# Two early loads of a convolution moved from SyncE's DMA queue to ScalarE's, behind a one-column copy

## The chip, the core and the metric

The kernel runs on one core of one Trainium2 chip. A core has five engines with instruction streams of their own: TensorE (PE; its weight loads are shown as PEld), VectorE (DVE), ScalarE (ACT), GpSimd (POOL) and SyncE (SP). TensorE multiplies and writes its results to PSUM; the others work elementwise or start transfers between HBM and SBUF. A DMA that an engine starts stands in that engine's queue; the transfers themselves run on 16 DMA engines. The metric is the device time of one execution in microseconds (us), lower is better.

## The reference

The input `x` is 16 x 64 x 64 x 64 (batch, channels in, height, width) in float32, the weight 128 x 64 x 3 x 3. Computed is a 3x3 convolution with a border of zeros, and behind it the maximum over blocks of 2 x 2:

```python
x_pad = np.pad(x, ((0, 0), (0, 0), (pad, pad), (pad, pad)))
for b, co, ci, kh, kw:
    conv[b, co] += weight[co, ci, kh, kw] * x_pad[b, ci, kh:kh+h, kw:kw+w]
for b, c, i, j:
    output[b, c, i, j] = np.max(conv[b, c, 2*i:2*i+2, 2*j:2*j+2])
```

The output is 16 x 128 x 32 x 32 in float32.

## The kernel before, in words

Two images lie in the 128 partitions at a time: 2 x 64 input channels. A matmul uses 64 partitions as its contraction, so matmuls for the two images run in pairs, on the two halves of TensorE's rows. The work is cut into 32 steps; a step is 16 rows of two images, hence 8 rows of pooled output, and each step has two halves `h`, one per image.

For two neighbouring rows the kernel doesn't compute both convolutions as they stand. It uses sums and differences of rows and of taps (the three weights of one row of the 3x3 window), so that fewer products are needed. There are two ways to do so. In a K step the differences are taken of the taps (D2 and D0) and TensorE reads the rows themselves in bfloat16 (`kx`) and a row sum (`ks`). In a W step differences of rows are made (`we` and `wd`, on VectorE or GpSimd) and a row sum `ws`, all from float32 rows in `wx`. Step 0 is a K step, step 1 a W step, step 2 a K step, step 3 a W step.

**The start.** Before a product can run, the weights must be loaded (`wraw`), combined and cast to bfloat16 (`wq`), turned by TensorE's transposes (lines 170) and copied back from PSUM to SBUF (`wt`, lines 182 to 188). The rows of step 0 are loaded as float32 into `kfirst` in two pieces: rows 0 to 8 (line 119) and rows 9 to 16 (line 120). ScalarE casts them to bfloat16 into `kx` (line 492). The first product of step 0 runs in two halves to match: F.0.0 needs the first piece, F.0.1 the second. `ksecond` (line 126) has the rows of step 2, cast at line 501. Step 1, the first W step, has its rows loaded in two parts by `wload(1, 0)` and `wload(1, 1)` (line 112); its differences `we` are made by halves too (Ea and Eb, line 393), and its `wd` at line 408. All these loads are issued by SP, in this order: wraw, kfirst's first piece, kfirst's second piece, ksecond, the two parts of step 1's rows. While they are under way TensorE runs eight matmuls on constants (line 595), whose results nobody reads.

**The order.** The order of instructions on every engine is written out by hand in the string `ORDER`: a name, a step and a half at a time (`EV` copies an accumulator out of PSUM, `MX` takes the maximum of two rows, `OD` copies the odd columns, `CM` takes the maximum of columns, `ST` stores, `L` loads rows, `LB` loads them behind the last VectorE instruction, `LK` loads rows for K steps by GpSimd's queue). Each engine executes its instructions in that order. On ScalarE the beginning is: cast of g0, casts of kfirst (XOa of the first piece; XOb and XEb of the second), a copy of turned taps (VG0), another cast of the first piece (XEa). On TensorE it is: transposes, F.0.0, F.0.1, transposes of D0, F.1.0, F.1.1, F.2.0 and so on. The instructions ahead of `ORDER` (the loads above, the memsets) come first on their engines. ScalarE's activation table is loaded by an instruction that the compiler puts ahead of ScalarE's first computation, which is the cast at line 194.

Of the kernel before, what the change touches and what calls it, by code (L numbers as in the profile page):

```python
# [11 lines left out]
def kernel(  # L12
# [9 lines left out]
    nc = tc.nc  # L22
    FP32 = mybir.dt.float32
    BF16 = mybir.dt.bfloat16
# [29 lines left out]
    const = ctx.enter_context(tc.tile_pool(name="const", bufs=1))  # L54
# [33 lines left out]
    def rows_of(p, lo, hi):  # L88
        return x[2 * p : 2 * p + 2].rearrange("b c h w -> (b c) h w")[:, lo:hi, :]

    def chunk(q):
        return (2 * R * q + (q > 0), min(H, 2 * R * (q + 1) + 1))

    NWX = 3
    kx = {}
    wx = [const.tile([128, H + 2, W], FP32, name=f"wx_{i}") for i in range(NWX)]
# [6 lines left out]
    def wload(s, part=None):  # L103
        p, q = place[s]
        lo, hi = chunk(q)
        if s == WSTEPS[0] and q > 0:
            lo = 2 * R * q - 1
        if part == 0:
            hi = 2 * R * q + R + 1
        elif part == 1:  # L110
            lo = 2 * R * q + R + 1
        return nc.sync.dma_start(out=wx[p % NWX][:, lo + 1 : hi + 1, :], in_=rows_of(p, lo, hi))

    wraw = const.tile([CO, CI * K * K], FP32)
    nc.sync.dma_start(out=wraw, in_=weight.rearrange("a b c d -> a (b c d)"))  # L115
    _, khi = chunk(0)
    kmid = R + 1
    kfirst = const.tile([128, khi, W], FP32)
    nc.sync.dma_start(out=kfirst[:, 0:kmid, :], in_=rows_of(0, 0, kmid))  # L119
    nc.sync.dma_start(out=kfirst[:, kmid:khi, :], in_=rows_of(0, kmid, khi))  # L120
    klo2, khi2 = chunk(1)
    ksecond = const.tile([128, khi2 - klo2, W], FP32)
    first_loads = (2, 1,)
    for s in first_loads:
        if s == KSTEPS[1]:
            nc.sync.dma_start(out=ksecond, in_=rows_of(0, klo2, khi2))
        else:
            wload(s, 0)
            wload(s, 1)
    zeros = const.tile([128, 512], BF16)  # L130
    nc.vector.memset(zeros, 0.0)
    ident = const.tile([128, 128], BF16)
    make_identity(nc, ident)
    for t in wx:
# [295 lines left out]
    def late_load(s):  # L430
        behind(wload(s), sbuf_op[0])
# [206 lines left out]
```

## Time and profile before

| | us |
|---|---|
| median of three runs | 104.66 (104.28 to 104.88) |
| the profiled execution | 104.47 |
| its span | 102.7 |
| TensorE busy | 96.2 (94% of the span) |
| VectorE, ScalarE, GpSimd busy | 91.6, 85.5, 77.9 |

The profile is one execution. Its span runs from the first to the last instruction that is shown; the 1.8 us between the span and the time of the execution lie around it. A line such as L492 is the line of the kernel that issued the instruction. SPq, ACTq and POOLq are the engines' DMA issues. In the list of DMA issues the last number is the time from the start of the issue until the data have landed, as the waiting instruction sees it. "Idle before" is time in which the engine stood still ahead of an instruction, with the event that ended it. TensorE's granted clock was full (1.00) in this profile throughout.

### The profile page before, as it was taken

How to read it: one execution, taken by the hardware profiler on the slowest of the kernel's cores; microseconds unless marked ns; L12 is line 12 of the kernel's file. 1: busy time of each engine (PE TensorE's matmuls, PEld its weight loads, DVE VectorE, ACT ScalarE, POOL GpSimd, SP SyncE). 2: the span in 40 equal slices, each digit the busy share in tenths (PEclk: the TensorE clock that was granted, in tenths of full speed). 3: DMA queues.
4: the chain of work that ended last, by engine and by line, in shares of the span. 5: the costliest groups of instructions: out<-in, count | busy, mean ns of one | idle time of the engine just before them, and what ended most of it. 6: DMA issues, size and time to landing. Idle time of an engine off the chain costs nothing.

```text
span 102.7 us, 2522 instructions
## 1 busy us (share of the span) xinstructions
PE 96.2 (94%) x905; PEld 54.3 (53%) x905; DVE 91.6 (89%) x176; ACT 85.5 (83%) x192; POOL 77.9 (76%) x66
## 2 busy tenths in 40 slices
PE   6969999999999999999999999999999999999920
PEld 2355465444454447655655555567657765555500
DVE  1576979999999999999999989999999999899960
ACT  4278697999889999997998899897989899897830
POOL 6262889995998799489959999789999688990000
PEclk9999999999999999999999999999999999999999
DMA  2989999999999999600538989930803673386553
GB/s 53 286 295 333 281 325 360 362 421 410 293 311 410 311 308 396 220 6 0 175 57 119 245 259 404 389 111 0 307 3 112 216 165 113 106 295 222 208 192 114
DMA packets 13341, 23.60 MB, mean 230 GB/s; under 512 B 1040, under 2 KB 9360, under 8 KB 13328
## 3 DMA queue, kind: packets, MB, share of 16 engines
q1 hardware_dynamic: 12464, 21.20, 58.8%
q0 software_dynamic: 720, 2.10, 11.6%
q8 instruction: 7, 0.11, 0.5%
q10 hardware_dynamic: 144, 0.13, 0.4%
q14 instruction: 6, 0.05, 0.1%
HBM read 17.14 MB, written 8.39 MB: 249 GB/s over the span
## 4 chain that ended last, share of the span: by engine, by line
PE 88%; DMA 4%; DVE 2%; SPq 1%; issue 1%; ACT 0%; DVEq 0%
PE acc L219 86%; DMA kfirst<-in_x_dram 4%; DVE o L477 1%; PE acc L170 1%; DVE acc L467 1%; PE acc L460 1%; SPq L119 0%; ACT kx L492 0%; SPq L115 0%; DVEq L633 0%
## 5 line engine op out<-in xcount | busy, mean ns | idle before, releaser
L219 PEld LDWEIGHTS <-wt 64*128 64x128 bf16 x870 | 51.7, 94 | 39.0 <-issue 2.0
L219 PE MATMUL acc<-wd,wt 64*128 64x504 bf16 (+3 forms) x276 | 54.4, 367 | 0.0
L381 POOL TENSOR_TENSOR wd<-wx 128x1024 bf16<-128x1024 f32 x21 | 49.2, 2360 | 4.5 <-DVE ws L360 2.0
L219 PE MATMUL acc<-kx,wt 64*128 64x504 bf16 (+6 forms) x264 | 44.7, 355 | 0.9 <-DVE wq L508 0.7
L467 DVE TENSOR_TENSOR acc<-acc,ev 128x512 f32<-128x512 f32 x64 | 42.0, 691 | 1.2 <-ACT ev L441 0.7
L219 PE MATMUL acc<-we,wt 64*128 64x512 bf16 (+3 forms) x138 | 32.5, 367 | 0.0
L219 PE MATMUL acc<-ws,wt 64*128 64x512 bf16 (+1 forms) x132 | 32.5, 377 | 0.0
L441 ACT ACTIVATE ev<-acc 128x512 f32<-128x512 f32 x44 | 26.3, 614 | 1.8 <-PE acc L219 1.3
L451 ACT COPY acc<-acc 128x512 f32<-128x512 f32 x42 | 24.5, 591 | 3.0 <-PE acc L219 1.8
L477 DVE TENSOR_TENSOR o<-acc,od 128x256 f32<-128x256 f32 x64 | 24.7, 416 | 0.9 <-ACT od L471 0.9
L471 ACT COPY od<-acc 128x256 f32<-128x256 f32 x64 | 22.8, 382 | 2.2 <-PE acc L219 1.7
L372 POOL TENSOR_TENSOR we<-wx 128x512 bf16<-128x512 f32 x16 | 20.1, 1272 | 4.0 <-PE acc L219 2.4
L219 PE MATMUL acc<-ks,wt 64*128 64x504 bf16 (+1 forms) x60 | 13.7, 377 | 0.0
L439 ACT COPY ev<-acc 128x512 f32<-128x512 f32 x20 | 11.7, 593 | 1.3 <-PE acc L219 1.2
L352 DVE TENSOR_REDUCE ws<-wx 128x512 bf16<-128x1024 f32 x9 | 11.1, 1232 | 0.0
L360 DVE TENSOR_TENSOR ws<-wx 128x512 bf16<-128x512 f32 x7 | 5.3, 766 | 0.0
L320 DVE TENSOR_TENSOR ks<-kx 128x512 bf16<-128x512 bf16 x10 | 4.3, 435 | 0.0
L408 POOL TENSOR_TENSOR wd<-wx 128x512 bf16<-128x512 f32 x2 | 2.5, 1264 | 2.2 <-DVE we L393 2.2
L339 DVE TENSOR_TENSOR ws<-wx,acc 128x512 bf16<-128x512 f32 x6 | 4.1, 675 | 0.0
L595 PE MATMUL acc<-const-bfloat16-1.0 128*128 128x512 bf16 x8 | 3.3, 582 | 0.8 <-PEq L619 0.8
L335 ACT COPY acc<-wx 128x512 f32<-128x512 f32 x6 | 3.6, 598 | 0.1
L372 DVE TENSOR_TENSOR we<-wx 128x512 bf16<-128x512 f32 x4 | 2.9, 749 | 0.3 <-DMA wx<-in_x_dram 0.3
(33 smaller groups left out, 26.6 us busy)
## 6 DMA issues: line engine op xcount, KB each, us to landing
out_dram<-o SPq DMA_DIRECT2D x31, 256.0 KB, 2.9
wx<-in_x_dram SPq DMA_DIRECT2D x10, 512.0 KB, 10.6
wx<-in_x_dram SPq DMA_DIRECT2D x6, 480.0 KB, 9.7
wx<-in_x_dram SPq DMA_DIRECT2D x5, 544.0 KB, 8.5
kx<-in_x_dram POOLq DMA_DIRECT2D x2, 528.0 KB, 7.5
ksecond<-in_x_dram SPq DMA_DIRECT2D x1, 512.0 KB, 6.4
kx<-in_x_dram POOLq DMA_DIRECT2D x1, 496.0 KB, 8.1
wx<-in_x_dram SPq DMA_DIRECT2D x1, 320.0 KB, 6.7
```

What stands on the lines that cost most here:

```text
L219: nc.tensor.matmul(acc[t][:, i0:i1, o0:o1], wt[lo : lo + CI, tap_of(m0, kw, h), :], rows(lo, i0, i1, c0, c1), start=start and kw == 1, sto ...
L320: nc.vector.tensor_tensor(out=row["ks", s], in0=t[:, f : f + 2 * R : 2, :], in1=t[:, f + 1 : f + 2 * R : 2, :], op=ADD)
L352: nc.vector.tensor_reduce(out=row["ws", s], in_=t[:, f : f + 2 * R, :].rearrange("p (r two) w -> p r w two", two=2), axis=mybir.AxisListTy ...
L360: nc.vector.tensor_tensor(out=row["ws", s], in0=t[:, f : f + 2 * R : 2, :], in1=t[:, f + 1 : f + 2 * R : 2, :], op=ADD)
L372: inst = (nc.vector if vector else nc.gpsimd).tensor_tensor(out=row["we", s], in0=t[:, f : f + 2 * R : 2, :], in1=t[:, f + 1 : f + 2 * R : ...
L381: nc.gpsimd.tensor_tensor(out=row["wd", s], in0=t[:, f + 1 : f + 1 + 2 * R, :], in1=t[:, f - 1 : f - 1 + 2 * R, :], op=SUB)
L439: nc.scalar.copy(out=ev[s, h], in_=acc[t])
L441: nc.scalar.mul(ev[s, h], acc[t], -1.0)
L451: nc.scalar.copy(out=acc[t], in_=acc[ta[s, h]])
L467: nc.vector.tensor_tensor(out=t, in0=t, in1=ev[s, h], op=MAX)
L471: nc.scalar.copy(out=od[s, h], in_=acc[tb[s, h]][:, :, 1::2])
L477: nc.vector.tensor_tensor(out=ot[s][:, h], in0=acc[t][:, :, 0::2], in1=od[s, h], op=MAX)
```

## The change

The second piece of `kfirst` and the first part of step 1's rows are issued by ScalarE in place of SP. Ahead of these two issues ScalarE gets a copy of one column of a constant into a tile that nobody reads, so the load of its table stands ahead of that copy and of the two issues. The memset of `zeros` on VectorE is moved to the front of the program. SP then issues wraw, kfirst's first piece, ksecond and the second part of step 1's rows. `ORDER` is unchanged, and so is the order of the computing instructions on every engine but for the added copy.

```diff
         elif part == 1:
             lo = 2 * R * q + R + 1
-        return nc.sync.dma_start(out=wx[p % NWX][:, lo + 1 : hi + 1, :], in_=rows_of(p, lo, hi))
-
+        queue = nc.scalar if part == 0 else nc.sync
+        return queue.dma_start(out=wx[p % NWX][:, lo + 1 : hi + 1, :], in_=rows_of(p, lo, hi))
+
+    zeros = const.tile([128, 512], BF16)
+    nc.vector.memset(zeros, 0.0)
+    primed = const.tile([128, 1], BF16)
+    nc.scalar.copy(out=primed, in_=nc.const_aps.tensor(1.0, [128, 1], BF16))
     wraw = const.tile([CO, CI * K * K], FP32)
     nc.sync.dma_start(out=wraw, in_=weight.rearrange("a b c d -> a (b c d)"))
     _, khi = chunk(0)
     kmid = R + 1
     kfirst = const.tile([128, khi, W], FP32)
     nc.sync.dma_start(out=kfirst[:, 0:kmid, :], in_=rows_of(0, 0, kmid))
-    nc.sync.dma_start(out=kfirst[:, kmid:khi, :], in_=rows_of(0, kmid, khi))
+    nc.scalar.dma_start(out=kfirst[:, kmid:khi, :], in_=rows_of(0, kmid, khi))
     klo2, khi2 = chunk(1)
     ksecond = const.tile([128, khi2 - klo2, W], FP32)
     first_loads = (2, 1,)
...
             wload(s, 0)
             wload(s, 1)
-    zeros = const.tile([128, 512], BF16)
-    nc.vector.memset(zeros, 0.0)
     ident = const.tile([128, 128], BF16)
     make_identity(nc, ident)
```

## The prediction

> **What bounds the kernel now.** I read the waits of TensorE (PE) first, because PE is busy 94% of the span and the question is only where it is not. Columns: who waited for what, total us, times, longest.
>
> ```profile
> PE acc L595 <- PEq L619: 0.8, 1, 0.8
> PE acc L219 <- DVE wq L508: 0.7, 1, 0.7
> PE acc L170 <- DVE wq L507: 0.2, 1, 0.2
> PE acc L219 <- ACT kx L492: 0.2, 1, 0.2
> ```
>
> Four waits, and no more in the whole run. Next I read the chain of work that ended last, for where they lie (start us, us, what).
>
> ```profile
> 1.65 4.30 DMA kfirst<-in_x_dram
> ...
> 5.98 0.41 ACT kx L492
> ...
> 6.43 0.50 PE acc L219 x6
> ...
> 12.27 84.18 PE acc L219 x785
> ```
>
> The chain goes through the second piece of kfirst: issued by SP at 1.65, landed 4.30 later at 5.95, cast by ScalarE (ACT) until 6.39, and the matmuls F.0.1 start at 6.43. Behind that PE never waits again. So whatever moves 6.43 moves the end by the same amount, as long as nothing later runs out of slack, and what stands before it costs nothing. The change touches exactly this stretch, so I read the start as a timeline (start, us, engine, line, what, idle before it):
>
> ```profile
> 0.74 1.28 ACT L194 ACT_TABLE_LOAD   x1 [0.74 <-PEq L619]
> ...
> 1.65 0.42 SPq L120 DMA_DIRECT2D kfirst<-in_x_dram  x1
> ...
> 2.11 0.43 SPq L126 DMA_DIRECT2D ksecond<-in_x_dram  x1
> 2.59 11.01 SPq L112 DMA_DIRECT2D wx<-in_x_dram  x11
> ...
> 3.59 0.53 ACT L194 CAST wq<-wraw 128x192 bf16<-128x192 f32 x1 [1.57 <-DMA wraw<-in_weight_dram]
> ...
> 4.24 0.83 PE L170 MATMUL acc<-ident,wq 128*128 128x128 bf16 x12 [0.19 <-DVE wq L507]
> ...
> 4.66 0.42 DVE L188 COPY wt<-acc 128x512 bf16<-128x512 bf16 x1 [0.16 <-PE acc L170]
> 5.00 0.75 DVE L508 TENSOR_TENSOR wq<-wraw 128x192 bf16<-128x192 f32 x1
> ...
> 5.31 0.41 ACT L492 CAST kx<-kfirst 128x256 bf16<-128x256 f32 x1 [1.19 <-DMA kfirst<-in_x_dram]
> ...
> 5.76 0.50 PE L219 MATMUL acc<-kx,wt 64*128 64x256 bf16 x6 [0.70 <-DVE wq L508]
> ```
>
> F.0.0 at 5.76 needs the first piece's cast (ends 5.72) and the taps that VectorE copied by 5.08. The wait is put down to L508, which ends at 5.75, but F.0.0 doesn't read its result: L508 makes D0, for the transposes behind F.0.1. So the first piece, cast from 5.31, held F.0.0, and the second held F.0.1 for 0.16 more. How fast the pieces came is in the DMA issues (KB, us to landing) and in half-microsecond windows (last column GB/s, before it the busy share of the 16 DMA engines):
>
> ```profile
> ksecond<-in_x_dram SPq DMA_DIRECT2D x1, 512.0 KB, 6.4
> wx<-in_x_dram SPq DMA_DIRECT2D x1, 320.0 KB, 6.7
> wraw<-in_weight_dram SPq DMA_DIRECT2D x1, 288.0 KB, 2.8
> kfirst<-in_x_dram SPq DMA_DIRECT2D x1, 288.0 KB, 4.1
> kfirst<-in_x_dram SPq DMA_DIRECT2D x1, 256.0 KB, 4.3
> ```
>
> ```profile
> 1.50:2.00 0.50, 0.50 (x2) 0.15 (x1) 0.00 (x0) 0.50 (x1) 0.50 (x7) 1.00 0.68 88
> 2.00:2.50 0.50, 0.50 (x3) 0.20 (x2) 0.00 (x0) 0.02 (x1) 0.27 (x4) 1.00 0.52 143
> 2.50:3.00 0.50, 0.50 (x3) 0.22 (x2) 0.00 (x0) 0.00 (x0) 0.00 (x0) 1.00 1.06 383
> 3.00:3.50 0.50, 0.50 (x3) 0.16 (x2) 0.00 (x0) 0.00 (x0) 0.00 (x0) 1.00 1.10 341
> 3.50:4.00 0.50, 0.50 (x2) 0.00 (x0) 0.41 (x1) 0.41 (x1) 0.00 (x0) 1.00 0.93 317
> 4.00:4.50 0.50, 0.31 (x6) 0.29 (x6) 0.50 (x2) 0.12 (x1) 0.00 (x0) 1.00 0.84 259
> 4.50:5.00 0.50, 0.50 (x11) 0.39 (x8) 0.34 (x2) 0.00 (x0) 0.42 (x1) 1.00 0.85 166
> 5.00:5.50 0.50, 0.07 (x2) 0.09 (x1) 0.50 (x2) 0.19 (x1) 0.39 (x1) 1.00 0.84 180
> 5.50:6.00 0.50, 0.24 (x6) 0.23 (x6) 0.50 (x2) 0.24 (x2) 0.00 (x0) 1.00 0.58 205
> ```
>
> Two readings. From 2.5 to 4.5 the DMA engines are full (share 0.84 to 1.10), so the early loads are held by the engines, not by SP's issuing. And landing is set by a late tail: summed, the windows give 849 kB by 5.0, where wraw and both pieces are 832 KB of 1024 bytes, 852 kB in all; the second piece landed only at 5.95, 0.9 after its mean share had moved. In 4.5 to 6.0 the rate falls to 166 to 205 GB/s, just where ksecond begins.
>
> **The change part by part.**
>
> *Zeros memset first, and the one-column copy.* The memset (0.27 us of VectorE, which otherwise idles until wraw lands) only changes its place in the program; on its engine it stays first: nothing. The copy and two issues occupy ACT in the 1.57 us it waits for wraw: the table load ends at 0.74 + 1.28 = 2.02; the copy has no row, its bounds are 0 and 0.41 (the 256-column cast), I take 0.2, nearer the lower end as it has one column; two issues at 0.42 with 0.05 between, as on SP, end at about 3.15. The cast of wraw starts at 3.59: covered by 0.4. Without that cover the cast and the transposes of g0 would slide, and those have until 5.76.
>
> *The second piece's issue.* It goes from 1.65 to 2.02 + 0.2 + 0.03 = 2.25, so 0.60 later (0.42 to 0.85 by the copy's bounds).
>
> *Its landing.* It has no row; it stands behind nothing in its new queue, but the 16 engines serve both queues. Lower end: as wraw, which ran alone, 2.8 after issue: 5.05. Upper end: wraw's first bytes move about 1.0 after its issue (first busy window 1.5 to 2.0), so the piece's bytes can move from 3.25. By then the windows give 392 kB: wraw and 97 kB of the first piece. If the queues alternate packet by packet (2048 B against 2304 B, later 4096 B of ksecond), the first piece's last 198 kB go with 176 kB of the second, and the second's last 86 kB with 172 kB of ksecond. The second is then done 172 kB later than in one queue; by the windows 852 kB are reached at about 5.02 and 1024 kB at 5.92, so 0.90 later: 6.85 with the same tail. I take the row nearest in kind, the first piece: it too had one load beside or ahead of it and landed in 4.1; 2.25 + 4.1 = 6.35, less 0.1 for 32 KB fewer: 6.25. That is 0.30 later than now.
>
> *The first piece.* It loses engine time to the second from 3.25 on. Bounds: earlier than 5.28, down to about 4.5, if its late tail is gone; later by what 176 kB take at 259 to 317 GB/s, 0.6. Up to 0.47 of it is free: F.0.0 may start at 6.23 if F.0.1 starts at 6.73. I take 0.2: no cost.
>
> *ksecond and the two W halves.* ksecond's issue moves from 2.11 to 1.65 on SP, the second W half from about 3.06 (2.59 + 0.42 + 0.05) to 2.11, the first from 2.59 to 2.72. ksecond now shares with the first W half, 320 KB, which at the 341 to 383 GB/s of full engines is up to 0.9; against it stand 0.46 of earlier issue. Its users have slack:
>
> ```profile
> 6.08 0.49 DVE L200 TENSOR_TENSOR wq<-gsum,wraw 128x192 bf16<-128x192 f32 x1
> ...
> 8.51 1.14 ACT L501 CAST kx<-ksecond 128x512 bf16<-128x512 f32 x2
> ...
> 9.32 0.43 DVE L393 TENSOR_TENSOR we<-wx 128x256 bf16<-128x256 f32 x1 [0.93 <-DMA wx<-in_x_dram]
> ...
> 9.93 1.15 PE L219 MATMUL acc<-kx,wt 64*128 64x256 bf16 x12
> ...
> 10.91 0.82 PE L219 MATMUL acc<-we,wt 64*128 64x256 bf16 x12
> ...
> 13.22 0.69 DVE L372 TENSOR_TENSOR we<-wx 128x512 bf16<-128x512 f32 x1 [0.32 <-DMA wx<-in_x_dram]
> ...
> 14.01 2.35 POOL L381 TENSOR_TENSOR wd<-wx 128x1024 bf16<-128x1024 f32 x1 [0.46 <-DVE we L372]
> ...
> 16.77 0.38 PE L219 MATMUL acc<-wd,wt 64*128 64x512 bf16 x1
> ```
>
> ksecond landed at 2.11 + 6.4 = 8.5, just as its casts began. They end at 9.65, and six of the twelve matmuls from 9.93 come ahead of the first that reads them, at about 10.35: 0.7 of slack, which grows with any delay of PE. Net cost nothing up to there. The first W half gates VectorE's difference at 9.32, done at 9.75 and read by PE at 10.91: slack 1.2. The next W load, in SP's queue behind these, is tied in the program to a VectorE tap sum (L200, ends 6.57), so SP's earlier slots don't reach it.
>
> *Sum.* F.0.1 starts at 6.25 + 0.03 + 0.41 + 0.04 = 6.73, 0.30 later than now. ACT's next casts and the copy of turned taps that F.1.0 needs shift alike, so nothing is caught up. The profiled execution took 104.47 (span 102.7): 104.77. It lies 0.19 under the median of the runs, 104.66, so for a median I say 104.95.
>
> [...]
>
> **The rivals.**
>
> *Slower: the second piece runs into ksecond's start.* Then the upper end holds: landing 6.85, F.0.1 at 7.33, +0.90: 105.56 as a median. For it: ksecond now starts right behind the first piece, and the windows from 4.5 show how little moves when it starts (166 GB/s at a busy share of 0.85). Against it: a stall in one queue may leave the engine free for the other. It decides once the piece lands after 6.45.
>
> *Slower: ACT isn't free at 2.02.* No row shows ACT computing between 2.02 and 3.59, so the copy may run as late as 3.59; then the piece is issued near 3.8 and lands between 6.6 (2.8 after) and 7.9 (4.1 after): +0.65 to +1.95, I take +1.0, 105.65. [...]
>
> *Faster: the late tails go.* If the second piece's engine time isn't stuck behind the first piece's stragglers, both land early. F.0.0 can't start before the transposes and the copied taps, 5.08, so F.0.1 is bounded by 5.14 + 0.50 = 5.64: at most 0.79. Beyond 0.41 step 3's row difference on GpSimd (ends 14.01 + 2.35 = 16.36, read at 16.77) must come earlier too, which its load, landed at 13.2 for the VectorE op, need not do. I take -0.6: 104.06. For it: 0.9 of the 4.30 is tail. Against: the piece starts 0.60 later and shares.
>
> **How the numbers follow.** Forecast 0.42, slower by ksecond 0.28, slower by ACT 0.08, faster 0.22. Half a per cent (0.52 us, about what a measurement of this kernel can tell from no change) bounds 104.14 and 105.18. The forecast's own range, 104.5 to 105.3, lies nearly all inside: same 0.39. Its upper edge and the two slow rivals give slower 0.41; the faster one lies mostly beyond the bound: 0.20. The range of 104.05 to 105.9 leaves a tenth at each side.
>
> **What would show it.** In the profile after: an issue on ACT's queue at 2.2 to 2.3; the second piece 4.0 after it; the first piece between 5.0 and 5.6; F.0.1's wait up from 0.16 while the wait before F.0.0 changes little; ksecond's casts no later than 9.2; and 84 us of unbroken matmuls behind. [...] A new PE wait behind 9.9 would make the sum wrong in a way I hold unlikely.

## The result and the profile after

The changed kernel took 106.15 us as a median (105.43 to 106.6), the kernel before 104.77 beside it; the ratio is 1.0124 with an interval of 1.008 to 1.0169. It is slower, above the range of the prediction (105.9), where I had forecast 104.95 and no measurable change. A ratio leaves out executions more than 1.5% above the fastest of their kernel, so where a kernel's executions lie in two groups I give the median and the ends as well.

The profiled execution after took 105.72, its span 103.9; before these were 104.47 and 102.7. TensorE's waits in the profile after (who waited for what: total us, times, longest):

```profile
PE acc L222 <- ACT kx L495: 1.3, 1, 1.3
PE acc L598 <- PEq L622: 0.8, 1, 0.8
PE acc L173 <- DVE wq L510: 0.7, 1, 0.7
```

The chain of work that ended last, after (start us, us, what):

```profile
1.18 5.50 DMA kfirst<-in_x_dram
6.67 0.02 issue
6.70 0.41 ACT kx L495
7.11 0.04 issue
7.15 0.83 PE acc L222 x12
7.98 0.33 PE acc L173 x4
...
13.30 84.22 PE acc L222 x785
```

Still no wait of TensorE behind the first products: the 84 us of matmuls begin at 13.30 in place of 12.27 and last as long. But the chain now goes through another load. Its issue at 1.18 is SP's, so it is the first piece of kfirst, which landed at 6.67 (5.28 before). F.0.0 and F.0.1 start together at 7.15 (twelve matmuls in one row), since the second piece had been there for long. The start, as a timeline of the changed kernel:

```profile
0.73 1.28 ACT L118 ACT_TABLE_LOAD   x1 [0.73 <-PEq L622]
...
0.80 0.39 ACTq L125 DMA_DIRECT2D kfirst<-in_x_dram  x1
...
1.18 0.42 SPq L124 DMA_DIRECT2D kfirst<-in_x_dram  x1
1.22 0.46 ACTq L113 DMA_DIRECT2D wx<-in_x_dram  x1
...
1.65 0.43 SPq L131 DMA_DIRECT2D ksecond<-in_x_dram  x1
...
2.03 0.19 ACT L118 COPY primed<-const-bfloat16-1.0 128x1 bf16<-128x1 bf16 x1
...
4.42 0.53 ACT L197 CAST wq<-wraw 128x192 bf16<-128x192 f32 x1 [2.19 <-DMA wraw<-in_weight_dram]
```

The two issues stand behind the table load and the copy in ScalarE's program, but they ran at 0.80 and 1.22, during the table load and before the copy at 2.03. These issues wait for no semaphore, and they didn't wait for the computing instructions ahead of them. So the first W part was issued 1.4 us earlier than before (1.22 against 2.59), ahead of ksecond, and almost with the first piece. The landings after (KB, us from issue to landing):

```profile
wx<-in_x_dram ACTq DMA_DIRECT2D x1, 320.0 KB, 6.3
wraw<-in_weight_dram SPq DMA_DIRECT2D x1, 288.0 KB, 3.7
kfirst<-in_x_dram SPq DMA_DIRECT2D x1, 288.0 KB, 5.5
kfirst<-in_x_dram ACTq DMA_DIRECT2D x1, 256.0 KB, 4.0
```

wraw landed near 4.4 (3.5 before), the second piece at 4.8 (5.95), the first at 6.67 (5.28). Both queues moved data at the same time: from 4.5 to 6.5, when the first piece was being fetched, ScalarE's queue had half of the 16 engines' time, and that was the W part. (Queue 10 is ScalarE's: packets, MB, share of the 16 engines.)

```profile
q10 hardware_dynamic: 133, 0.30, 51.7%
q1 hardware_dynamic: 128, 0.35, 45.5%
```

The four transposes of D0 behind F.0.1, from the timelines of before and of after, give the whole shift:

```profile
6.87 0.40 PE L170 MATMUL acc<-ident,wq 128*128 128x128 bf16 x4
```

```profile
7.92 0.40 PE L173 MATMUL acc<-ident,wq 128*128 128x128 bf16 x4
```

It is 1.05. Of that, 0.72 is the last piece's later landing (6.67 against 5.95). The other 0.33 comes from the order: as the last piece is now the first one, F.0.0 no longer runs while the second is awaited, and from the start of the products that wait for the last piece to the transposes it is 0.77 (from 7.15) in place of 0.44 (from 6.43). The rest of the 1.25 between the profiled executions lies in the last stores and outside the span, and isn't explained.

That is one pair of executions. The changed kernel was profiled once more, in an execution of 105.18; there the first piece landed at 6.22 and the same transposes started at 7.46, 0.59 later than before:

```profile
6.24 1.02 ACT L495 CAST kx<-kfirst 128x256 bf16<-128x256 f32 x3 [1.61 <-DMA kfirst<-in_x_dram]
...
7.46 0.40 PE L173 MATMUL acc<-ident,wq 128*128 128x128 bf16 x4
```

Again the first piece, the last one to land, held the products, but the shift is little more than half as large.

### The profile page after: what moved, and what is told of

Read it like the earlier page. It is cut to its first block, busy times and chain, and to the rows that moved or that the text cites. A ratio compares the mean times of both kernels' runs of the same rounds, so it can differ in the third digit from the quotient of the medians.

```text
span 103.9 us, 2523 instructions
## 1 busy us (share of the span) xinstructions
PE 96.4 (93%) x905; PEld 54.6 (53%) x905; DVE 91.6 (88%) x176; ACT 85.6 (82%) x193; POOL 78.0 (75%) x66
## 4 chain that ended last, share of the span: by engine, by line
PE 87%; DMA 5%; DVE 2%; issue 1%; ACT 0%; SPq 0%; DVEq 0%
PE acc L222 85%; DMA kfirst<-in_x_dram 5%; DVE o L480 1%; PE acc L173 1%; DVE acc L470 1%; PE acc L463 1%; ACT kx L495 0%; SPq L120 0%; DVEq L636 0%
## 5 line engine op out<-in xcount | busy, mean ns | idle before, releaser
L510 DVE TENSOR_TENSOR wq<-wraw 128x192 bf16<-128x192 f32 x1 | 0.5, 499 | 3.3 <-DMA wraw<-in_weight_dram 3.3
```

## The experiments

The diffs are against the changed kernel, but for the extra load, which is against the kernel before.

**One moved load at a time.** First the second piece alone, with the W part back in SP's queue:

```diff
-        queue = nc.scalar if part == 0 else nc.sync
+        queue = nc.sync
```

> Only the second piece of kfirst goes through ScalarE's queue; the first W part is back in SP's. Theory: ScalarE issues at about 0.8, without waiting for its table or its copy, so the piece's 262 kB share the 16 DMA engines with wraw, and wraw lands near 4.4 as in the changed kernel (4.42). The first piece then shares with ksecond and nothing else: it lands between 5.28 (before) and 6.67 (changed), at about 5.8. F.0.0 then starts near 6.3 and F.0.1 near 6.75: +0.3 us against before, clearly less than the changed kernel's +1.2. Rival (the lateness is a random stall of one DMA engine, not sharing): wraw lands at 3.5 or the first piece varies freely, and the time is that of before or of the changed kernel. Rival (it is the copy or the issues on ScalarE): the time is as the changed kernel's, +1.2.

Measured: 104.59 (104.45 to 105.02), ratio 1.0008 (0.999 to 1.0026). No loss at all. Its timeline:

```profile
4.22 0.53 ACT L197 CAST wq<-wraw 128x192 bf16<-128x192 f32 x1 [2.00 <-DMA wraw<-in_weight_dram]
...
4.87 0.83 PE L173 MATMUL acc<-ident,wq 128*128 128x128 bf16 x12 [0.90 <-DVE wq L510]
...
5.68 1.02 ACT L495 CAST kx<-kfirst 128x256 bf16<-128x256 f32 x3 [0.93 <-DMA kfirst<-in_x_dram]
...
6.14 0.83 PE L222 MATMUL acc<-kx,wt 64*128 64x256 bf16 x12 [0.44 <-ACT kx L495]
...
6.90 0.40 PE L173 MATMUL acc<-ident,wq 128*128 128x128 bf16 x4
```

wraw is late as expected (4.2), but the first piece lands at 5.66, earlier than I expected (5.8), and the transposes of D0 start at 6.90, where they started before. The products need wraw and both pieces, 852 kB, and here it made no difference in which order these three came. The window from 4.5 to 6.0 (last column GB/s) shows why it isn't later: the first row is of the kernel before.

```profile
4.50:6.00 1.50, 0.80 (x17) 0.72 (x15) 1.34 (x3) 0.43 (x2) 0.81 (x1) 1.00 0.76 184
```

```profile
4.50:6.00 1.50, 0.83 (x12) 0.78 (x13) 1.34 (x4) 0.57 (x3) 0.79 (x1) 1.00 1.02 393
```

The dip at ksecond's start, 184 GB/s, isn't there in that stretch with a load in the second queue. What the dip is, no run settles.

Then the W part alone:

```diff
-    nc.scalar.dma_start(out=kfirst[:, kmid:khi, :], in_=rows_of(0, kmid, khi))
+    nc.sync.dma_start(out=kfirst[:, kmid:khi, :], in_=rows_of(0, kmid, khi))
```

> Only the first W part goes through ScalarE's queue, the second piece stays in SP's. Theory: 328 kB that nobody needs before 9.3 us share the engines with wraw and the first piece from the start. wraw lands near 4.4, the first piece near 5.8, the second behind it near 6.5; F.0.1 starts near 7.0: +0.5 us (0.3 to 0.9). Rival (random stalls): as before. Rival (ScalarE's copy and issue): +1.2.

Measured: 106.02 (105.86 to 107.26), ratio 1.016 (1.008 to 1.024). The whole loss, and more than the 0.3 to 0.9 us that I expected. With the piece gone from ScalarE's queue the W part is issued at 0.80, earlier still than in the changed kernel. Twelve transposes took 1.33 in its profile and 0.83 in the others above, to which I come back.

```profile
0.80 0.39 ACTq L113 DMA_DIRECT2D wx<-in_x_dram  x1
...
5.04 1.33 PE L173 MATMUL acc<-ident,wq 128*128 128x128 bf16 x12 [0.69 <-DVE wq L510]
...
6.76 0.40 ACT L495 CAST kx<-kfirst 128x256 bf16<-128x256 f32 x1 [1.84 <-DMA kfirst<-in_x_dram]
...
7.22 0.50 PE L222 MATMUL acc<-kx,wt 64*128 64x256 bf16 x6 [0.85 <-ACT kx L495]
...
7.43 0.71 ACT L495 CAST kx<-kfirst 128x256 bf16<-128x256 f32 x2 [0.27 <-DMA kfirst<-in_x_dram]
```

The pieces land near 6.7 and 7.4. And neither moved load, but the rest of the change:

```diff
-        queue = nc.scalar if part == 0 else nc.sync
+        queue = nc.sync
...
-    nc.scalar.dma_start(out=kfirst[:, kmid:khi, :], in_=rows_of(0, kmid, khi))
+    nc.sync.dma_start(out=kfirst[:, kmid:khi, :], in_=rows_of(0, kmid, khi))
```

> All loads in SP's queue as before; only the one-column copy and the earlier memset are added. Theory: nothing, within 0.3 us of before; wraw lands at 3.5, the first piece near 5.3. Rival (the copy on ScalarE costs): +0.2 or more.

Measured: 104.8 (104.26 to 105.1), ratio 1.0022 (0.9995 to 1.0049). The copy and the memset cost nothing that can be told. In its profile, of its slowest execution, the second piece landed at 6.44 and the first at 4.5, in the kernel before at 5.95 and 5.28, with the same loads in the same queue: landings of one arrangement differed by 0.5 to 0.8 us between these two executions. The 6.44 is even later than the 6.22 at which the last piece landed in the changed kernel's second profile. So shifts between single profiles show by which way a loss can come, but not how large it is; for that the times over all executions count. This profile shows one thing more. Its twelve transposes took 1.39, about as long as in the W part's run, though TensorE had hardly idled ahead of them (the constants end at 4.35):

```profile
4.42 1.39 PE L173 MATMUL acc<-ident,wq 128*128 128x128 bf16 x12
```

**The time of the issue.** The prediction had ScalarE issue at 2.25. That can be had with a semaphore:

```diff
-    nc.scalar.copy(out=primed, in_=nc.const_aps.tensor(1.0, [128, 1], BF16))
+    primer = nc.scalar.copy(out=primed, in_=nc.const_aps.tensor(1.0, [128, 1], BF16))
...
-    nc.scalar.dma_start(out=kfirst[:, kmid:khi, :], in_=rows_of(0, kmid, khi))
+    behind(nc.scalar.dma_start(out=kfirst[:, kmid:khi, :], in_=rows_of(0, kmid, khi)), primer)
```

> As the changed kernel, but the second piece's issue waits on a semaphore for the copy's end, so that ScalarE's two issues start at about 2.3, as my prediction had it. Theory: wraw is through before the second piece moves (3.3) and lands near 3.6; the first piece shares and lands at 5.3 to 5.9; the second at about 6.25; F.0.1 near 6.7: +0.3 us, and clearly less than the changed kernel. If the time stays at +1.2, the time of the issue isn't what matters, and the theory of sharing by early issue falls.

Measured: 109.38 (108.33 to 109.81), ratio 1.0435 (1.0342 to 1.0529). The time of the issue matters, but the other way: by this run, had ScalarE done what I predicted, the kernel would have been far slower.

```profile
2.25 0.38 ACTq L125 DMA_DIRECT2D kfirst<-in_x_dram  x1
...
5.29 0.50 PE L222 MATMUL acc<-kx,wt 64*128 64x256 bf16 x6
...
8.71 0.71 ACT L495 CAST kx<-kfirst 128x256 bf16<-128x256 f32 x2 [3.83 <-DMA kfirst<-in_x_dram]
...
9.17 0.82 PE L222 MATMUL acc<-kx,wt 64*128 64x256 bf16 x6 [3.38 <-ACT kx L495]
```

The second piece landed at 8.69, 6.4 after its issue, though it was alone at the head of its queue. The DMA queues from 2.25 to 5.2 and from 5.2 to 6.2 show when it moved:

```profile
q1 hardware_dynamic: 362, 0.92, 88.9%
```

```profile
q1 hardware_dynamic: 85, 0.20, 64.0%
q10 hardware_dynamic: 47, 0.10, 25.6%
```

For 3 us after its issue not one packet of ScalarE's queue was moved (in the changed kernel, issued at 0.80, its packets began at 2.6). ksecond, issued at 1.66 in the other queue, landed ahead of it, near 8.4. So here the two queues weren't served packet by packet from the moment of the issue, as I had assumed. The simplest reading is that loads are begun in the order of their issue over both queues, and that those issued close together share; it is a reading, not shown by itself. The half and half from 4.5 to 6.5 in the changed kernel (133 packets of ScalarE's queue, 128 of SP's) fits it, as the first piece and the W part had been issued at 1.18 and 1.22. What held the second piece back for these 3 us, no row here shows.

The same wait on the W part's issue alone, with the second piece at 0.80, turns that into a prediction:

```diff
-            wload(s, 0)
+            behind(wload(s, 0), primer)
```

> As the changed kernel, but the first W part's issue waits for the copy's end, so that it starts at about 2.3 and not at 1.2; the second piece is issued at 0.8 as in the changed kernel. Theory now (both queues are served as one, in the order of issue; what counts is the bytes issued ahead of the last of wraw and the two pieces): ksecond (1.65) and the second W part (2.12) come ahead of the first W part, nothing but 852 kB ahead of the pieces; the first piece lands at about 5.7 as with the second piece alone on ScalarE, and the time is that of before, within 0.4 us. Rival (two queues share packet by packet, whenever they were issued): the W part still takes bandwidth from the first piece as soon as it is issued, and 0.5 us or more of the loss stays.

Measured: 104.66 (104.5 to 106.57), ratio 1.0016 (0.9989 to 1.0043). Both loads are in ScalarE's queue as in the changed kernel, and the loss is gone.

```profile
0.80 0.38 ACTq L125 DMA_DIRECT2D kfirst<-in_x_dram  x1
...
2.25 0.33 ACTq L113 DMA_DIRECT2D wx<-in_x_dram  x1
...
5.47 1.02 ACT L495 CAST kx<-kfirst 128x256 bf16<-128x256 f32 x3 [0.58 <-DMA kfirst<-in_x_dram]
```

The first piece is there at 5.47 instead of 6.67. The W part, issued at 2.25, landed 6.1 later, near 8.4, behind ksecond, which was issued at 1.66 and landed near 6.8; in the changed kernel, issued at 1.22, it had landed near 7.5, ahead of ksecond (8.5). This bears out the reading above. wraw was as late as in the changed kernel (4.36 against 4.42), so it is not wraw that carries the loss. One execution of the ten took 106.57; it wasn't profiled. This wait and the three runs with one moved load or none settle the cause together: the W part was issued ahead of its turn.

**The cost of a load by itself.** The kernel before with one more load at the start, issued by ScalarE and read by nobody:

```diff
+    extra = const.tile([128, 8, W], FP32)
+    nc.scalar.dma_start(out=extra, in_=rows_of(7, 40, 48))
     wraw = const.tile([CO, CI * K * K], FP32)
```

> The kernel before, with nothing moved, and one load more: 262 kB of rows that nobody reads, issued by ScalarE at 0.75. It is the disputed cost by itself. Theory: the second piece now has 1114 kB issued up to it in place of 852 kB; it lands about 0.9 later (0.6 to 1.3), wraw lands near 4.3 and the time is +0.9 us (0.6 to 1.4). Rival (the loss of the changed kernel comes from which queue the pieces are in): within 0.3 us of before.

Measured: four executions at 104.47 to 104.69 and six at 106.04 to 106.52, a median of 106.09; the ratio of 1.0028 (0.9975 to 1.0081) comes mostly from the first four, while the median lies 1.6 us above the 104.46 beside it. In the profile, of an execution in the lower group, 262 kB more put wraw back to 4.6 but the second piece only to 6.2, 0.25 later and not 0.9: there the expectation fell. The DMA engines moved 402 GB/s from 4.5 to 5.5, where the kernel before had 166 and 180, so most of the extra load seems to have fitted into the dip:

```profile
4.50:5.50 1.00, 0.22 (x5) 0.26 (x6) 0.87 (x2) 0.60 (x2) 0.00 (x0) 1.00 1.05 402
```

The gap between the groups, 1.35 us at the least, can't be read from that one profile; the next runs bear on it.

**The copy.** Without it ScalarE's table load stands behind the issues:

```diff
-    primed = const.tile([128, 1], BF16)
-    nc.scalar.copy(out=primed, in_=nc.const_aps.tensor(1.0, [128, 1], BF16))
```

> The changed kernel without the one-column copy; ScalarE's table load now stands behind its two issues. Theory: the issues start at about 0.75 instead of 0.80, the table is loaded by 2.9 at the latest and is needed at 4.4; the time is that of the changed kernel, +1.2 us (0.9 to 1.6). Rival (the copy holds or costs something): the time differs from the changed kernel's by more than 0.4 us.

Measured: 106.54 (106.34 to 106.75), ratio 1.0199 (1.0144 to 1.0254), against 1.0124 of the changed kernel with intervals that overlap. The first piece landed at 6.2, earlier than in the changed kernel's profile, and wraw 0.3 later, but TensorE was slow:

```profile
5.36 1.44 PE L171 MATMUL acc<-ident,wq 128*128 128x128 bf16 x12 [1.01 <-DVE wq L508]
6.73 1.46 PE L220 MATMUL acc<-kx,wt 64*128 64x256 bf16 x12
```

The same two rows took 0.83 each in the changed kernel's profile. By the spacing of its matmuls, TensorE ran at half its rate until 9.7. It started at half rate in every kernel here: the constants took 0.43 each at first, and 0.23 each where fourteen of them stand behind F.0.0 in a later kernel (3.23 in all). It reached the full rate between 3.4 and 6.4 us in twelve of the fourteen profiles, and later in two, this one and that of the swapped pieces below (9.1). In these two and in seven others all eight constants ran at half rate (3.57 for the eight, 3.27 in the kernel before). In the two TensorE then idled for 1.0 and 0.9 us ahead of the transposes, in the seven for 0.71 or less.

Where TensorE had already left the half rate, idling of that length didn't bring it back: with the extra load it idled 1.26 behind constants of which the last ran at full rate, and the transposes still took 0.83.

```profile
5.28 0.83 PE L172 MATMUL acc<-ident,wq 128*128 128x128 bf16 x12 [1.26 <-DVE wq L509]
```

Nor was idling needed for half rate at the transposes, as the kernel with the copy alone showed (1.39). What two profiles against seven suggest is that 0.9 us and more of idling, before the full rate is reached, puts it off by some 3 us. The clock column doesn't show any of this: it reads 1.00 from 4.5 to 11.5 in these two, and over all of the start in the kernel before, so that the full clock named ahead of the prediction is the column's, not that of the first constants. In the kernel of 109.38, with full rate at the transposes (0.83) and 3.4 us of idling after F.0.0, the half rate did come back, and the column has it (third column from the right):

```profile
9.00:14.00 5.00, 4.83 (x42) 2.61 (x43) 1.96 (x6) 2.89 (x7) 0.00 (x0) 0.50 1.00 297
```

The column fell from 1.00 to 0.50 between 7.0 and 7.5 (0.79 over that half microsecond), 1.2 to 1.7 us after F.0.0's end at 5.79, and was back at 1.00 from 15 to 16. How long TensorE must idle for this, one such run doesn't show, nor does it show why the executions of one kernel lie in two groups.

**The pieces swapped between the queues.** The first piece through ScalarE, all else through SP:

```diff
-    nc.sync.dma_start(out=kfirst[:, 0:kmid, :], in_=rows_of(0, 0, kmid))
-    nc.scalar.dma_start(out=kfirst[:, kmid:khi, :], in_=rows_of(0, kmid, khi))
+    nc.scalar.dma_start(out=kfirst[:, 0:kmid, :], in_=rows_of(0, 0, kmid))
+    nc.sync.dma_start(out=kfirst[:, kmid:khi, :], in_=rows_of(0, kmid, khi))
```

with the W part in SP's queue as well.

> The first piece goes through ScalarE's queue at 0.8, the second and both W parts through SP's. Theory: 852 kB up to the second piece, as before, so F.0.1 can't start before about 6.1 to 6.4; wraw shares with the first piece and lands near 4.3, which puts F.0.0 at 5.9 or later. Within 0.4 us of before, perhaps 0.2 faster as the queue behind has no gap. Rival (a faster start of two queues is worth something): 0.4 us or more faster.

Measured: seven executions at 104.48 to 104.84, three at 106.0 to 106.65; ratio 1.0038 (0.9998 to 1.0078). No gain. The profile is of one of the three, 106.16, and it shows what sets that one apart:

```profile
5.24 1.44 PE L173 MATMUL acc<-ident,wq 128*128 128x128 bf16 x12 [0.89 <-DVE wq L510]
6.61 1.46 PE L222 MATMUL acc<-kx,wt 64*128 64x256 bf16 x12
```

Both pieces had landed by 6.2, but the long row of matmuls began at 13.83 in place of 12.27, with TensorE at half rate until 9.1. So in this execution the loss is TensorE's rate. In the four kernels whose lower executions are as fast as the kernel before, the number of executions above 106 goes with the start of the transposes in the one profile of each: none of ten at 4.87 (second piece alone), one at 5.01 (W part issued at 2.25), three at 5.24 (pieces swapped), six at 5.28 (extra load). That is a hint, not a proof, as the other upper executions weren't profiled.

**TensorE kept busy.** More matmuls on constants where TensorE would idle, first in the changed kernel:

```diff
-        g0 D2 ... TG2 g1 F.0.0 F.0.1 TD0
+        g0 D2 ... TG2 g1 KB.4 F.0.0 KB.0 F.0.1 TD0
...
+    def keep_busy(times):
+        for _ in range(times):
+            nc.tensor.matmul(
+                acc[7].rearrange("p a b -> p (a b)"), ones[:, 0:128], ones, start=True, stop=True, skip_group_check=True
+            )
+
+    steps["KB"] = keep_busy
     for n in range(8):
...
+    keep_busy(3)
```

> The changed kernel, with three more matmuls on constants behind the eight at the start and four more ahead of F.0.0, into a bank that nobody reads, so that TensorE hardly idles while it waits for the loads. Theory (two costs: the loads land late, and the longer idle stretch behind the first matmuls keeps TensorE at half its rate for some us in part of the executions): the loads' cost stays, +0.7 to +1.2 us, but no execution is near 106.5; all lie in 105.1 to 105.9. Rival (the spread of the changed kernel, 105.4 to 106.6, is in the landing of its loads): the spread stays.

Measured: 105.58 (104.95 to 106.23), ratio 1.0098 (1.0061 to 1.0136). The changed kernel itself ran beside it:

> The changed kernel itself, beside the three above on the same chip. Both theories: about 1.0 to 2.0 us over the kernel before; if the half rate comes and goes, executions in two groups, near 105.5 and near 106.6.

Measured: 106.34 (105.18 to 107.14), ratio 1.0123 (1.0054 to 1.0192). The highest times are gone, but a spread of 1.3 us stays and the intervals overlap, so my expectation of 105.1 to 105.9 fell. Four of the ten lie at 106.04 to 106.23; none of these was profiled, so what sets them apart is open. That 1.0% of 1.2% stays with TensorE kept busy points to the loads for most of the loss, without showing it. In the other two it was clearer. Without the copy, with three and two matmuls more:

> The changed kernel without the one-column copy (106.5), with three more matmuls on constants at the start and two ahead of F.0.0. Theory: in its profile the first products took 1.40 us for twelve where other kernels show 0.83, and the transposes 1.44 against 0.83; with TensorE kept busy they take 0.83 and the time falls to 105.2 to 105.8, as the changed kernel's. Rival (the copy matters for itself, by the table load's place): it stays at 106.5.

Measured: 105.37 (104.87 to 105.72), ratio 1.0066 (1.0035 to 1.0098), 1.2 us under the same kernel without these matmuls (1.4 by the ratios, since the two ran on different chips). The products are back at full rate, the transposes ahead of them in part (1.21 for twelve):

```profile
7.07 0.83 PE L220 MATMUL acc<-kx,wt 64*128 64x256 bf16 x12
```

And the kernel with the late second piece, with fourteen matmuls on constants between F.0.0 and F.0.1:

> The kernel whose second piece waits for the copy's end (109.4), with fourteen matmuls on constants (3.0 us at 0.216) between F.0.0 and F.0.1. Theory: F.0.1 still starts near 9.2, 2.7 us later than before, but at full rate: 107.0 to 107.6, so that about 2 us of its loss are TensorE's half rate. Rival: it stays near 109.4 and the loss is all in the loads.

Measured: 107.44 (106.99 to 107.95), ratio 1.0271 (1.0215 to 1.0327): 1.9 us of its 4.8 (1.7 by the ratios) were TensorE's rate, the rest, 2.8, the wait. In this profile the second piece was cast by 8.72, but the added matmuls held TensorE until F.0.1 at 9.16, so up to 0.4 of that rest is their own.

No kernel tried was faster than the one before.

## Why the prediction was wrong

- **What bounds the kernel** held. Nothing behind the first products waits; what moves them moves the end: 1.03 us at the start of the long row of matmuls, 1.07 at the last maximum (0.58 at the start of the row in the second profile).
- **The copy** was sized right (0.19 against 0.2) and started where I said (2.03). But *the second piece's issue*, put at 2.02 + 0.2 + 0.03 = 2.25, is the step that failed first: it ran at 0.80, and the W part's, put at 2.72, at 1.22. I took a DMA issue for an instruction that waits for the ones ahead of it on its engine. The trace of before had no row that showed the one or the other, and my bounds, 0.42 to 0.85 later than before, covered only the length of the copy; an earlier issue wasn't in them.
- **ksecond and the two W halves, "net cost nothing".** This is the step that carries the loss. With its issue at 1.22 the W part came ahead of ksecond and beside the first piece; moved alone it costs 1.6%, taken out or issued at 2.25 the loss is gone. I had only asked what its own users lose, not whom it pushes back.
- **The first piece, "I take 0.2: no cost".** It landed 1.39 later, 0.94 in the second profile, and became the gate. Its upper bound of 0.6 was the second piece's 176 kB; the W part wasn't in it.
- **Its landing.** The second piece landed at 4.8, below the lower end of 5.05, by its early issue. The sharing packet by packet on which my upper end rested didn't hold for an issue at 2.25: there none of its packets moved before 5.2, where I had the first at 3.25, and it landed at 8.69, beyond that end by 1.8. The two errors went opposite ways.
- **The rivals.** Landing past 6.45 gave +0.90 in the rival by ksecond, near the number, but by another piece and another load: what it names didn't happen, since ksecond was issued behind the W part. ScalarE not being free is refuted by the copy's row: it started at 2.03, 0.02 after the table load's end, and not as late as 3.59. The faster rival didn't come: the dip at 4.5 to 6.0 did go when a load was moved, but the W part's bytes took its place.
- **Open.** How the changed kernel's loss divides. Both of its profiled executions ran their first products at full rate (0.83 for twelve), so their shifts of 1.05 and 0.59 are the loads alone; but these are two of its faster executions, and those above 106 have no profile. They may have TensorE at half rate, as the slow execution of the swapped pieces had, or later loads. What remains of the spread when TensorE is kept busy isn't explained either.

## What to carry to other kernels

A load moved to another engine's queue is moved in time as well (here from 1.65 to 0.80 and from 2.59 to 1.22): look at when that engine issues it in the trace, not at what stands ahead of it in the program, and if it is to come later, give it a wait (here it took the loss away for the W part; for the second piece, which the first products need, it cost 4.4%). At the start, where the DMA engines are full (a busy share of 0.77 to 1.07 from 2.5 to 4.5 in the changed kernel), sort the loads of all queues together by the time of their need: the W part, first read at 9.36, delayed a piece that ScalarE awaited from 4.95 on. How much such a load costs isn't set by its bytes alone: the extra load of 262 kB delayed the second piece by only 0.25 in the one profile. A wait that is lengthened ahead of TensorE's first products seems to cost its rate too in part of the executions (twelve transposes took 1.44 in place of 0.83 behind 0.9 and 1.0 us of idling), so compare the duration of equal matmuls, not only the clock column.

## What the runs showed of the hardware that I had not expected

- DMA issues of ScalarE at 0.80 and 1.22 ran during its table load (0.73 to 2.01) and ahead of a copy that stood before them in the program.
- A load at the head of its own queue, issued at 2.25, moved no packet until 5.2 while loads issued earlier in the other queue were served.
- TensorE at half its rate (1.46 us for twelve matmuls that take 0.83) with the clock column at 1.00; with wraw as late, five more matmuls on constants gave the products the full rate (0.83).
- The end of TensorE's half rate at the start differs from profile to profile, 3.4 to 6.4 us in twelve of them, 9.1 and 9.7 in two.
